# Turning attention probabilities eight at a time instead of four in a streaming Conformer layer

## Chip, cores and metric

One core of a Trainium2 chip runs the whole layer. The metric is device time in microseconds (us) of one execution; a version is timed several times and compared by the median.

## What is computed

One layer of a streaming encoder over 2048 prompt frames and 64 sample frames of width 1024, all in float32: a normalised input goes through one projection into a gated pair for a convolution branch, queries, keys and values, and two gates; the two branches are merged by the gates, projected and added; a gated feed-forward part follows. The attention branch is banded: each chunk of 64 frames reads itself and the 8 chunks before it, with 8 heads of 64 channels.

```python
q = rms_norm(q.reshape(B, T, N_HEADS, HEAD_DIM), p['q_norm_g'])
k = rms_norm(k.reshape(B, T, N_HEADS, HEAD_DIM), p['k_norm_g'])
o = attend(q, k, v, p['rel_bias']).reshape(B, T, ATTN_DIM)
...
s = jnp.einsum('bqhd,bkhd->bhqk', q, k).astype(jnp.float32) * ATTN_SCALE
s = s + rel_bias[:, rel].astype(jnp.float32)[None]
s = jnp.where(mask[None, None], s, NEG_INF)
p = jax.nn.softmax(s, axis=-1).astype(v.dtype)
return jnp.einsum('bhqk,bkhd->bqhd', p, v)
...
merged = jax.nn.sigmoid(g_conv) * conv_out + jax.nn.sigmoid(g_attn) * attn_out
x = x + gt1 * (merged @ p['w_o'])
```

## The kernel before

**Number format.** TensorE multiplies float32 data as a high part and a rest, so a projection step is a triple of matmuls (high by high, rest by high, high by rest; in the trace `ps<-hh,whi`, `ps<-hl,whi`, `ps<-hh,wlo`, or the same with the operands exchanged). A tile that TensorE is to read is split first: ScalarE copies it into the rounded high part, VectorE subtracts that from the source and writes the rest.

**Stages.** Phase one (0 to about 1163 us of the span) takes the prompt in four blocks of frames (0 to 3), each with its norm, its projections for queries, keys, values, gated pair and gates, the convolution and the attention of 8 heads; block 0 has the 8 sample heads too. Between the blocks of projections some steps of the modulation (`pa<-wmod,cl`) are put. Phase two merges the branches (`ps<-cin`, gated tiles `t<-tg,ps`), projects, and runs the feed-forward part. Attention results go to DRAM as `o_d`, the convolution's normalised channels (`ln`) as `c_d`; both are split into the tiles `part_h` and `part_l` by `parts()`, a ring of two buffers that the storing of normalised keys uses too. Tiles of phase two take memory of phase one, so the first of them wait for the last stores.

**What sets the order.** The program is written out by Python generators. Each attention head is a generator `attend(i)` in a lane; while the projections are being written, `stream.tick` lets lanes put in a step whenever a model of the engines' load says that the step's inputs are ready. A bare `yield` gives the projections the next turn; `yield t` waits until the model's TensorE time reaches `t`. In phase one TensorE runs in the order in which the kernel writes its matmuls (a schedule given by hand for that engine alone); the order on VectorE, ScalarE, GpSimd (POOL) and SyncE (SP) is set by the tile scheduler.

**One prompt head.** For four tiles of 128 queries: scores (`sc<-kk,q`, one PSUM tile), reduction with bias on VectorE (`pr,sm<-sc,bias`), exponential and scaling on ScalarE. Then the probabilities are turned: for each group `jj` in `seq`, TensorE transposes up to four 128 x 128 pieces of `pr` into one PSUM tile `ptp`, `split` copies it into `ph` and `pl` (three buffers each), and the group goes to the list `pend`. `av` multiplies a group with the values into `po`. Heads of blocks 1 to 3 have five groups of four transposes (`seq` 3, 4, 0, 1, 2); heads of block 0 have four groups of 4, 3, 2 and 1. `ptp` shares a pool of five PSUM banks (tag `gp`) with the projections `ps`, the norm's and the keys' transposes `pt`, and the modulation's `pa`.

**Keys.** Each key tile is normalised (`kn<-kn,r` on VectorE), transposed on TensorE (`pt<-ident,kn`) at least 5 us of model time later, split and stored.

**Lines.** Every compute instruction is recorded through a helper, so all of them have line L105 in the trace, and the tiles' names tell them apart. L1350 stores the convolution's channels, L1460 a pair of heads.

Of the kernel before, what the change touches and what calls it, by code (L numbers as in the profile page):

```python
# [8 lines left out]
F32 = mybir.dt.float32  # L9
# [7 lines left out]
P = 128  # L17
# [605 lines left out]
def streaming_layer(ctx: ExitStack, tc: tile.TileContext, I, O):  # L623
    nc = tc.nc
    stream = Stream()
    pe, dve, act, gps = (
        Meter(e, n, stream) for e, n in ((nc.tensor, "pe"), (nc.vector, "dve"), (nc.scalar, "act"), (nc.gpsimd, "pool"))
    )
# [28 lines left out]
    ident = const.tile([P, P], F32, name="ident")  # L657
# [118 lines left out]
    ps_g = p1.enter_context(tc.tile_pool(name="ps_g", bufs=5, space=PSUM))  # L776
# [6 lines left out]
    def temp(name, shape=(P, 512)):  # L783
        return wk.tile(list(shape), F32, tag="t", name=name, bufs=NT)
# [679 lines left out]
    def spans(b):  # L1464

        if b == "s":
            return 0, SMP, 0, CACHE + SMP
        past = QB if b else 0
        return SMP + QB * b, QB, CACHE + SMP + QB * b - past, QB + past
# [19 lines left out]
    def fetch_qk(i):  # L1489
        if i < len(order) and ("qk", i) not in now:  # L1490
            x, h = order[i]
            if spare["open"]:
                spare["heads"].append(i)
            now["qk", i] = load_qk(x, h, *spans(x))

    def fetch(i):
        if i < len(order) and i not in loaded:
            x, h = order[i]
            fetch_qk(i)
            if now["bias"] is None or now["bias"][0] != h:  # L1500
                now["bias"] = h, load_bias(h)
            first = not i or x not in ("s", 0, order[i - 1][0])
            lag = FIRST_LAG if first else QK_LAG
            loaded[i] = max(stream.load["pe"] + BIAS_LAG, ahead_qk.get(i, stream.load["pe"] + lag))

    def fetch_v(i):
        if i < len(order) and ("v", i) not in now:
            x, h = order[i]
            now["v", i] = load_v(h, *spans(x)[2:])

    def attend(i):
        x, h = order[i]
        q0, nq, k0, nk = spans(x)
        yield lambda: now["scored"] == i - 1
        fetch(i)
        fetch_v(i)
        if not i:
            fetch_qk(1)
        yield loaded[i]
        if i + 1 < len(order) and (spare["open"] or i in spare["heads"]):  # L1520
            fetch_qk(i + 1)
            ahead_qk[i + 1] = stream.load["pe"] + QK_LAG
        (q2, kk), (_, bias), vnow = now["qk", i], now["bias"], now["v", i]
        tiles = []
        for t in range(0, nq, P):
            n = min(P, nq - t)
            if x not in (0, "s"):
                ps = ps_a.tile([P, 2, 512], F32, tag="s", name="sc")
                for j in range(2):
                    for d in range(2):  # L1530
                        pe.matmul(ps[:, j, :320], q2[:, d, t : t + P], kk[:, t + 320 * j : t + 320 * j + 320], start=d == 0, stop=d == 1)
                w, src, bs = 640, ps[:, :, :320], bias[:, ::-1]
            else:
                w = nk if x == "s" else t + P

                if "banks" not in now:
                    sc = ps_a.tile([P, 2, 512], F32, tag="s", name="sc")
                    now["banks"] = [sc[:, 0:1], sc[:, 1:2]]
                ps = now["banks"].pop(0)
                now["banks"].append(ps)  # L1540
                for d in range(2):
                    pe.matmul(ps[:n, 0, :w], q2[:, d, t : t + n], kk[:, :w], start=d == 0, stop=d == 1)
                src, bs = ps[:n, 0:1, :w], bias[:n, 64:384][:, ::-1] if x == "s" else bias[:, :w][:, ::-1]
            pr, sm, free, ready = softmax_max(src, n, w, bs)
            tiles.append((pr, sm, n, w))
            if t + P < nq:
                yield free + PE_LAG, SCORE_ROOM
            else:
                fetch(i + 1)
                if (x, order[min(i + 2, len(order) - 1)][0]) in ((0, 0), ("s", "s")):  # L1550
                    fetch_qk(i + 2)
                now["scored"] = i
            if t:
                softmax_scale(*tiles[-2], x in ON_ACT)
        yield ready
        softmax_scale(*tiles[-1], x in ON_ACT)
        yield stream.when("act" if x in ON_ACT else "dve") + PE_LAG
        while now["finished"] < i - 1:
            yield lambda: now["finished"] == i - 1
        fetch_v(i + 1)  # L1560
        po = ps_a.tile([P, 512], F32, tag="o", name="po")
        if x == "s":
            pt = ps_g.tile([P, 512], F32, tag="gp", name="ptp")
            ph = wk.tile([P, 512], F32R, tag="ph", name="ph", bufs=3)
            pl = wk.tile([P, 512], F32R, tag="pl", name="pl", bufs=3)
            js = ((0, P), (1, P), (2, SMP))
            for j, m in js:
                c = slice(j * SMP, j * SMP + SMP)
                pe.transpose(pt[:m, c], tiles[0][0][:SMP, j * P : j * P + m], ident[:SMP, :SMP])
            stream.after("act", "pe")  # L1570
            split(ph[:, : 2 * SMP], pl[:, : 2 * SMP], pt[:, : 2 * SMP])
            split(ph[:SMP, 2 * SMP : 3 * SMP], pl[:SMP, 2 * SMP : 3 * SMP], pt[:SMP, 2 * SMP : 3 * SMP])
            yield stream.when("dve") + PE_LAG
            for j, m in js:
                c = slice(j * SMP, j * SMP + SMP)
                for y_ in (ph, pl):
                    pe.matmul(po[:, :SMP], vnow[:m, j], y_[:m, c], start=j == 0 and y_ is ph, stop=j == 2 and y_ is pl)
        else:
            seq = (0, 1, 2, 3) if x == 0 else (3, 4, 0, 1, 2)

            def av(jj, ph, pl, _):
                if x:
                    uses = [(jj, 0, min(jj, 3) + 1)] + ([(jj + 5, jj + 1, 4)] if jj < 3 else [])
                else:
                    uses = [(jj, jj, 4)]
                for j, a, e in uses:
                    for y_ in (ph, pl):
                        pe.matmul(
                            po[:, a * P : e * P], vnow[:, j], y_[:, a * P : e * P], start=jj == seq[0] and y_ is ph,
                            stop=jj == seq[-1] and y_ is pl and j == uses[-1][0], skip_group_check=True,  # L1590
                        )

            pend = []
            for jj in seq:
                if len(pend) > 2:
                    yield pend[0][3] + PE_LAG
                    av(*pend.pop(0))
                pt = ps_g.tile([P, 512], F32, tag="gp", name="ptp")
                t0 = 0 if x else jj
                for t in range(t0, 4):  # L1600
                    j = (jj - t + (5 if t > jj else 0)) if x else jj
                    pe.transpose(pt[:, t * P : t * P + P], tiles[t][0][:, j * P : j * P + P], ident)
                ph = wk.tile([P, 512], F32R, tag="ph", name="ph", bufs=3)
                pl = wk.tile([P, 512], F32R, tag="pl", name="pl", bufs=3)
                stream.after("act", "pe")
                w = 512 - t0 * P
                if x in ON_POOL and jj % 2:
                    p32 = temp("p32")
                    act.activation(p32[:, :w], pt[:, t0 * P :], AF.Copy)
                    act.activation(ph[:, t0 * P :], p32[:, :w], AF.Copy)  # L1610
                    stream.after("pool", "act")
                    gps.tensor_tensor(pl[:, t0 * P :], p32[:, :w], ph[:, t0 * P :].bitcast(F32), ALU.subtract)
                    pend.append((jj, ph, pl, stream.when("pool")))
                else:
                    split(ph[:, t0 * P :], pl[:, t0 * P :], pt[:, t0 * P :])
                    pend.append((jj, ph, pl, stream.when("dve")))
                yield
            for args in pend:
                yield args[3] + PE_LAG
                av(*args)  # L1620
        yield stream.when("pe")
        yield from finish_head(h, po, SMP if x == "s" else QB, q0, "s" if x == "s" else "p")
        now["finished"] = i
# [95 lines left out]
    ps_g = ctx.enter_context(tc.tile_pool(name="ps_c", bufs=4, space=PSUM))  # L1719
# [184 lines left out]
    for s, (lo, hi) in enumerate(CBLOCKS):  # L1904
        tiles = token_tiles(lo, hi)
# [476 lines left out]
```

## Time and profile before

| | |
|---|---|
| median of three runs | 2945.97 us (2940.69 to 2946.77) |
| profiled execution | 2941.67 us |
| its span, instructions | 2939.5 us, 44832 |
| mean granted TensorE clock | 0.997 |
| busy: PE, DVE, ACT, POOL | 98%, 70%, 46%, 40% |

PE is TensorE's matmuls, PEld its weight loads, DVE VectorE, ACT ScalarE. A row of the timeline has the start in us from the span's start, the length in us, the engine, the line, the operation and its tiles as output<-inputs, the shape, and how many instructions are run together; brackets hold the idle time before it and what ended that.

### The profile page before, as it was taken

The numbers are of one execution on the slowest core, as the hardware profiler recorded it, in microseconds if no ns is written. First come the engines' busy times: TensorE is split into PE (matmuls) and PEld (weight loads), VectorE is DVE, ScalarE is ACT, GpSimd is POOL, SyncE is SP. The second block draws the span as 40 slices with busy tenths as digits, with TensorE's granted clock in tenths as the row PEclk, the third lists the DMA queues.
The fourth block names the chain that finished last, engine by engine and source line by source line (L and its number), as shares of the span: only waits on it lengthen the run. The fifth ranks groups of instructions, "written<-read, shape, count | busy, mean of one in ns | idle before, by whom it ended". The sixth has DMA issues, their size and how long they took to land.

```text
span 2939.5 us, 44832 instructions
## 1 busy us (share of the span) xinstructions
PE 2889.3 (98%) x16193; PEld 2587.5 (88%) x16193; DVE 2053.9 (70%) x3648; ACT 1362.7 (46%) x2453; POOL 1164.9 (40%) x753
## 2 busy tenths in 40 slices
PE   7999999999999999999999999999999999999999
PEld 5899777888888887988999998999999999999998
DVE  5897788668967885577777756666666557566666
ACT  3346543751564266563444345444444345444442
POOL 1201210111011002553566452366567742465667
PEclk9999999999999999999999999999999999999999
DMA  9989899978996987984444875332333965333333
GB/s 322 315 305 314 287 281 329 285 232 306 285 297 197 320 270 224 291 295 157 144 144 146 292 261 200 97 122 94 115 115 104 346 220 179 97 103 106 115 107 127
DMA packets 467067, 628.04 MB, mean 214 GB/s; under 512 B 36196, under 2 KB 314584, under 8 KB 466845
## 3 DMA queue, kind: packets, MB, share of 16 engines
q1 hardware_dynamic: 452944, 606.11, 63.4%
q10 hardware_dynamic: 13901, 19.08, 1.9%
q8 instruction: 127, 2.08, 0.3%
q14 instruction: 95, 0.78, 0.1%
HBM read 476.53 MB, written 148.54 MB: 213 GB/s over the span
## 4 chain that ended last, share of the span: by engine, by line
PE 47%; DVE 2%; ACT 1%; DMA 1%; issue 1%; POOL 0%; SPq 0%; ACTq 0%; DVEq 0%; POOLq 0%
PE ps L105 29%; PE pd L105 13%; PE pw L105 5%; DVE wlo L105 1%; ACT whi L105 1%; DVE ps L105 0%; DMA cin<-o_d 0%; DMA x<-x_d 0%; DVE acc L105 0%; ACT xn L105 0%; DMA wst<-in_w_ffn_in 0%; DMA wfo<-in_w_ffn_out 0%; DMA tg<-g_d 0%; DVE sums L105 0%; PE pt L105 0%
## 5 line engine op out<-in xcount | busy, mean ns | idle before, releaser
L105 PE MATMUL ps<-t,whi 128*128 128x384 f32 (+1 forms) x2112 | 502.0, 322 | 2.8 <-ACT u L105 1.7
L105 POOL TENSOR_TENSOR wlo<-wst,whi 128x1024 fp32r<-128x1024 f32 (+1 forms) x159 | 362.7, 2293 | 246.1 <-ACT whi L105 214.4
L105 ACT ACTIVATE whi<-wst 128x1024 fp32r<-128x1024 f32 (+1 forms) x265 | 258.3, 979 | 316.1 <-PE ps L105 129.6
L105 PE MATMUL ps<-b,whi 128*128 128x384 f32 (+1 forms) x1584 | 380.7, 325 | 6.4 <-DVE v L105 2.1
L105 PEld LDWEIGHTS ps<-t,whi 128*128 128x128 f32 x2112 | 367.8, 188 | 10.1 <-ACT u L105 3.9
L105 DVE SCALAR_TENSOR_TENSOR y<-u,wd,y 128x512 f32<-128x512 f32 (+1 forms) x480 | 370.1, 774 | 8.0
L105 PE MATMUL ps<-hh,whi 128*128 128x512 f32 (+2 forms) x992 | 362.8, 366 | 0.1
L105 DVE TENSOR_TENSOR acc<-acc,pd 128x512 f32<-128x512 f32 x482 | 322.2, 685 | 48.1 <-PE pd L105 45.6
L105 PE MATMUL ps<-hh,wlo 128*128 128x512 f32 (+2 forms) x992 | 345.2, 348 | 0.0
L105 PE MATMUL ps<-hl,whi 128*128 128x512 f32 (+2 forms) x992 | 344.5, 347 | 0.0
L105 PE MATMUL ps<-t,wlo 128*128 128x384 f32 (+1 forms) x1056 | 338.5, 321 | 0.0
L105 PE MATMUL pd<-whi,hid 128*128 128x512 f32 x912 | 297.9, 391 | 0.6 <-DVE hid L105 0.3
L105 PEld LDWEIGHTS ps<-b,whi 128*128 128x128 f32 x1584 | 276.9, 188 | 14.6 <-DVE v L105 3.2
L105 ACT ACTIVATE pr<-pr,sm 128x640 f32<-128x640 f32 (+3 forms) x272 | 201.9, 749 | 137.1 <-DVE sm L105 134.8
L105 PE MATMUL ps<-b,wlo 128*128 128x384 f32 (+1 forms) x792 | 256.1, 323 | 0.0
L105 POOL TENSOR_TENSOR r<-t,mhalf 128x1 f32<-128x1 f32 (+2 forms) x68 | 82.3, 1219 | 403.7 <-DVE t L105 377.8
L105 PEld LDWEIGHTS ps<-hh,wlo 128*128 128x128 f32 x992 | 186.5, 188 | 22.6
L105 DVE TENSOR_TENSOR wlo<-wst,whi 128x1024 fp32r<-128x1024 f32 (+1 forms) x106 | 135.9, 1286 | 100.3 <-ACT whi L105 98.9
L105 PEld LDWEIGHTS pd<-whi,hid 128*128 128x128 f32 x912 | 171.2, 188 | 37.2 <-DVE acc L105 1.8
L105 PEld LDWEIGHTS ps<-hh,whi 128*128 128x128 f32 x992 | 187.0, 189 | 18.2 <-issue 3.3
L105 PEld LDWEIGHTS ps<-hl,whi 128*128 128x128 f32 x992 | 187.4, 189 | 14.3 <-issue 1.7
L105 PEld LDWEIGHTS ps<-t,wlo 128*128 128x128 f32 x1056 | 198.2, 188 | 0.8
(233 smaller groups left out, 6309.6 us busy)
## 6 DMA issues: line engine op xcount, KB each, us to landing
whi<-w_din_h SPq DMA_DIRECT2D x72, 512.0 KB, 6.4
wlo<-w_din_l SPq DMA_DIRECT2D x72, 512.0 KB, 7.3
wst<-sum_d SPq DMA_DIRECT2D x131, 256.0 KB, 3.1
wfo<-in_w_ffn_out SPq DMA_DIRECT2D x64, 512.0 KB, 4.1
wmod<-in_w_ada SPq DMA_DIRECT2D x46, 512.0 KB, 8.8
sum_d<-ws SPq DMA_DIRECT2D x88, 256.0 KB, 2.0
wst<-in_w_ffn_in SPq DMA_DIRECT2D x85, 256.0 KB, 3.2
wst<-in_w_in SPq DMA_DIRECT2D x40, 512.0 KB, 6.0
```

Source lines behind the costliest of these rows:

```text
L105: self.last = f(*args, **kw)
```

## The change

The transposes of two groups are put into TensorE's order back to back, in two PSUM tiles, and both are split before the head gives up its turn: runs of eight, of seven and three in block 0, and of four for a fifth group alone. `turned` holds the second tile of a pair. The list of waiting groups is shortened before a new pair: if two groups wait, and the group to come has not been turned and is not the last, the oldest is multiplied first. A head of blocks 1 to 3 has three turns instead of five, one of block 0 two instead of four. Which transposes, splits and products there are stays the same.

```diff
-            pend = []
+            def turn_probs(jj):
+                pt = ps_g.tile([P, 512], F32, tag="gp", name="ptp")
+                for t in range(0 if x else jj, 4):
+                    j = (jj - t + (5 if t > jj else 0)) if x else jj
+                    pe.transpose(pt[:, t * P : t * P + P], tiles[t][0][:, j * P : j * P + P], ident)
+                return pt
+
+            pend, turned = [], {}
             for jj in seq:
-                if len(pend) > 2:
+                if len(pend) > 2 or len(pend) == 2 and jj not in turned and jj != seq[-1]:
                     yield pend[0][3] + PE_LAG
                     av(*pend.pop(0))
-                pt = ps_g.tile([P, 512], F32, tag="gp", name="ptp")
-                t0 = 0 if x else jj
-                for t in range(t0, 4):
-                    j = (jj - t + (5 if t > jj else 0)) if x else jj
-                    pe.transpose(pt[:, t * P : t * P + P], tiles[t][0][:, j * P : j * P + P], ident)
+                if jj not in turned:
+                    turned.update({i: turn_probs(i) for i in seq[seq.index(jj) :][:2]})
+                pt, t0 = turned.pop(jj), 0 if x else jj
                 ph = wk.tile([P, 512], F32R, tag="ph", name="ph", bufs=3)
                 pl = wk.tile([P, 512], F32R, tag="pl", name="pl", bufs=3)
...
-                yield
+                if not turned:
+                    yield
```

Since a head's steps come at other times, the steps of the other lanes move too, and the tile scheduler sets other orders on the other engines. Three places follow.

TensorE in block 2, one head before the change:

```order
L105 MATMUL ptp<-ident,pr 128x128 x4
L105 MATMUL ps<-hh,whi 128x512
L105 MATMUL ps<-hl,whi 128x512
L105 MATMUL ps<-hh,wlo 128x512
L105 MATMUL ptp<-ident,pr 128x128 x4
L105 MATMUL ps<-hh,whi 128x512
L105 MATMUL ps<-hl,whi 128x512
L105 MATMUL ps<-hh,wlo 128x512
L105 MATMUL ptp<-ident,pr 128x128 x4
```

The start of the same kind of head after it:

```order
L105 MATMUL ptp<-ident,pr 128x128 x8
L105 MATMUL ps<-hh,whi 128x512
L105 MATMUL ps<-hl,whi 128x512
L105 MATMUL ps<-hh,wlo 128x512
L105 MATMUL ps<-hh,whi 128x512
L105 MATMUL ps<-hl,whi 128x512
L105 MATMUL ps<-hh,wlo 128x512
L105 MATMUL ps<-hh,whi 128x512
L105 MATMUL ps<-hl,whi 128x512
L105 MATMUL ps<-hh,wlo 128x512
L105 MATMUL po<-ph,vv 128x512
L105 MATMUL po<-pl,vv 128x512
```

Eight transposes stand together, and the first product follows three projection triples behind them.

VectorE at the seam between block 0 and block 1, before (names carry their buffers' numbers; kn_4027 is the key tile that TensorE transposes first, kn_4095 a later one):

```order
L105 TENSOR_TENSOR kn_4095<-kn_4095,r_4166 128x512
L105 ISA pr_4254,sm_4255<-sc_1921,bias_194 128x384
L105 ISA sm_4255 128x1
L105 TENSOR_SCALAR u_4131<-tb_4183,ps_4185 128x512
L105 RECIPROCAL sm_4243<-sm_4243 128x1
L105 TENSOR_SCALAR y_4130<-u_4131,wd_178,cols_175 128x512
L105 RECIPROCAL sm_4255<-sm_4255 128x1
L105 COPY R_4276<-pa_4259 128x256
L105 TENSOR_TENSOR part_l_4119<-ln_4114,part_h_4118 128x512
L105 TENSOR_TENSOR part_l_4127<-ln_4122,part_h_4126 128x512
L105 TENSOR_SCALAR part_l_4152<-pt_4146,gqk_179,part_h_4151 128x512
L105 TENSOR_TENSOR kn_4027<-kn_4027,r_4041 128x512
```

VectorE there after the change (kn_4126 is the last of the three key tiles, which now come in TensorE's order):

```order
L105 ISA pr_4209,sm_4210<-sc_1921,bias_194 128x256
L105 ISA sm_4210 128x1
L105 RECIPROCAL sm_4210<-sm_4210 128x1
L105 ISA pr_4231,sm_4232<-sc_1921,bias_194 128x384
L105 ISA sm_4232 128x1
L105 TENSOR_TENSOR kn_4126<-kn_4126,r_4159 128x512
```

The key tile stands directly behind the reduction of a 128 x 384 score tile, where before eleven instructions stood between the reduction's neighbour kn_4095 and kn_4027.

TensorE at the same seam after the change:

```order
L105 MATMUL pt_4298<-ident_160,kn_4126 128x128 x4
L105 MATMUL ptp_4308<-ident_160,pr_4167 128x128
L105 MATMUL ptp_4308<-ident_160,pr_4209 128x128
L105 MATMUL ptp_4308<-ident_160,pr_4231 128x128
L105 MATMUL ptp_4308<-ident_160,pr_4261 128x128
L105 MATMUL ptp_4313<-ident_160,pr_4209 128x128
L105 MATMUL ptp_4313<-ident_160,pr_4231 128x128
L105 MATMUL ptp_4313<-ident_160,pr_4261 128x128
L105 MATMUL pa_4326<-wmod_610,cl_192 32x256 x4
L105 MATMUL pa_4326<-wmod_612,cl_192 32x256 x4
```

A pair of four and three transposes follows the key tile's, and the modulation's first matmul stands directly behind the pair.

VectorE at the end of phase one, before:

```order
L105 TENSOR_TENSOR pl<-ptp,ph 128x512 x5
L105 TENSOR_TENSOR o_p<-other,po 64x512
L105 TENSOR_SCALAR y<-y,cols 128x512
L105 TENSOR_SCALAR ln<-ln,y 128x512
L105 TENSOR_TENSOR part_l<-o_p,part_h 128x512
L105 TENSOR_TENSOR part_l<-ln,part_h 128x512
L105 TENSOR_SCALAR ps<-tg,ps 128x320
L105 TENSOR_TENSOR part_l<-ln,part_h 128x512
L105 TENSOR_SCALAR t_12594<-tg,ps 128x320
```

And after:

```order
L105 TENSOR_SCALAR y<-y,cols 128x512
L105 TENSOR_SCALAR ln<-ln,y 128x512
L105 TENSOR_TENSOR pl<-ptp,ph 128x512 x2
L105 COPY row<-pt 32x128
L105 TENSOR_TENSOR pl<-ptp,ph 128x512 x3
L105 TENSOR_TENSOR o_p<-other,po 64x512
L105 TENSOR_TENSOR part_l<-o_p,part_h 128x512
L105 TENSOR_TENSOR part_l<-ln,part_h 128x512
L105 TENSOR_SCALAR ps<-tg,ps 128x320
L105 TENSOR_SCALAR t_12594<-tg,ps 128x320
```

One `part_l<-ln` stands behind the last head's result `o_p` where two stood.

## Prediction

> **What bounds the kernel now.** I read the page first, then TensorE's waits in the stretch that holds the changed step, a table of stretches, and the timeline where TensorE waits long. Busy time and the chain of waits:
>
> ```profile
> span 2939.5 us, 44832 instructions
> PE 2889.3 (98%) x16193; PEld 2587.5 (88%) x16193; DVE 2053.9 (70%) x3648; ACT 1362.7 (46%) x2453; POOL 1164.9 (40%) x753
> PE 47%; DVE 2%; ACT 1%; DMA 1%; issue 1%; POOL 0%; SPq 0%; ACTq 0%; DVEq 0%; POOLq 0%
> ```
>
> TensorE is busy for 98% of the span and holds the chain wherever it has an owner. The change takes no matmul from it, so it can only win or lose where TensorE waits or runs slowly. Columns of the table: length, busy us (instructions) of each engine, granted clock, DMA share, GB/s.
>
> ```profile
> core 0: us, PE busy (x) PEld busy (x) DVE busy (x) ACT busy (x) POOL busy (x), PEclk, DMA share, GB/s
> 345.00:365.00 20.00, 16.04 (x95) 11.88 (x93) 12.69 (x30) 8.38 (x20) 0.55 (x2) 0.91 0.89 298
> 365.00:385.00 20.00, 20.00 (x94) 16.71 (x93) 18.99 (x37) 8.21 (x18) 3.64 (x2) 0.91 0.94 289
> 600.00:1110.00 510.00, 509.32 (x2777) 430.81 (x2775) 395.46 (x749) 243.30 (x445) 57.10 (x51) 1.00 0.85 274
> 1150.00:1160.00 10.00, 9.28 (x51) 7.50 (x50) 5.81 (x13) 9.03 (x17) 2.37 (x1) 1.00 0.25 86
> 1170.00:1175.00 5.00, 1.87 (x13) 1.61 (x11) 2.62 (x2) 0.00 (x0) 1.82 (x1) 0.89 0.43 134
> 1175.00:1185.00 10.00, 9.71 (x49) 9.71 (x50) 3.73 (x10) 2.88 (x4) 3.18 (x2) 0.71 0.95 297
> ```
>
> From 600 to 1110 us, where most of the regrouped heads run, TensorE idles 0.68 us in 510: nothing is to be had there. Two places are left, the seam between the first two blocks of frames (345 to 385) and the step from attention into the merge (1160 to 1185). TensorE's waits between 180 and 1260 (total, times, longest) name them:
>
> ```profile
> PE pt L105 <- DVE kn L105: 4.0, 1, 4.0
> PE ps L105 <- DVE t L105: 3.4, 1, 3.4
> PE pa L105 <- DMA wmod<-in_w_ada: 2.6, 4, 0.7
> PE po L105 <- DVE pl L105: 0.8, 3, 0.3
> PE ptp L105 <- ACT pr L105: 0.7, 2, 0.5
> ```
>
> Only the first two are followed by a lower clock (0.91 twice; 0.71).
>
> **The change, part by part. (a) The grouping.**
>
> ```profile
> 781.74 0.60 PE L105 MATMUL ptp<-ident,pr 128*128 128x128 f32 x4
> 782.87 0.60 PE L105 MATMUL ptp<-ident,pr 128*128 128x128 f32 x4
> ...
> 784.58 0.39 PE L105 MATMUL ps<-hh,whi 128*128 128x512 f32 x1
> ...
> 785.28 0.39 PE L105 MATMUL ps<-hh,whi 128*128 128x512 f32 x1
> 1137.79 1.03 PE L105 MATMUL ptp<-ident,pr 128*128 128x128 f32 x8
> 1139.36 0.60 PE L105 MATMUL ptp<-ident,pr 128*128 128x128 f32 x4
> ```
>
> Four transposes and a projection triple take 782.87 − 781.74 = 1.13 us from start to start, a triple alone 785.28 − 784.58 = 0.70, so four transposes cost 0.43. Eight stand together once already: with a triple 1139.36 − 1137.79 = 1.57, so eight cost 0.87 = 2 × 0.435. The 64 runs that disappear are worth 64 × (0.87 − 2 × 0.43) = 0.6 us at the rounding of the rows, either way. I take 0.
>
> **(b) The wait for kn goes.** The key heads' tiles kn leave VectorE in the opposite order to the one TensorE wants:
>
> ```profile
> 353.04 0.69 DVE L105 TENSOR_TENSOR kn<-kn,r 128x512 f32<-128x512 f32 x1
> 359.68 0.68 DVE L105 TENSOR_TENSOR kn<-kn,r 128x512 f32<-128x512 f32 x1
> 360.51 0.63 PE L105 MATMUL pt<-ident,kn 128*128 128x128 f32 x4 [3.96 <-DVE kn L105]
> ```
>
> The transposes at 360.51 take the tile written at 359.68; the one of 353.04 is wanted only later. In the changed order VectorE writes the three kn tiles in TensorE's order, and the last one directly behind a score reduction, 24 projection matmuls ahead of its use: 8 triples × 0.70 = 5.6 us, against 0.69 for the multiply. So the 3.96 goes, and what would be late next is the split in (c). The clock was 0.91 over two stretches of 20 us, which costs up to 2 × 20 × 0.09 = 3.6. Together −7.6; ends −7.6 and 0 (if VectorE reaches that multiply 6 us late).
>
> The Trainium skill ("TensorE: Matmul & The Clock Gate", Part 1) has the gate fall to half clock after an idle window of about 3.4 us and rise after a busy one as long. The trace agrees that only the waits of 3.96 and 3.42 were followed by a lower clock. By that rule an estimate of each loss is half of 3.4, or 1.7, not the rows' 3.6 and 2.9, and the sum below would be 3.1 weaker: 2938.4.
>
> **(c) A new wait at the same seam.** In the changed order TensorE there runs four kn transposes, then a pair of four and three probability transposes, and directly behind them the first matmul pa of the next modulation step, which takes the PSUM bank of the pair's first tile. That bank is free after its split, a ScalarE copy and a VectorE subtraction (durations shortest/median/longest, in ns):
>
> ```profile
> L105 ACT ACTIVATE ph<-ptp x168: 199/584/609, 194.4 to 1161.2; 128x512 fp32r<-128x512 f32 x128, 128x128 fp32r<-128x128 f32 x16, 128x384 fp32r<-128x384 f32 x8, 128x256 fp32r<-128x256 f32 x8
> L105 DVE TENSOR_TENSOR pl<-ptp,ph x168: 205/687/693, 196.4 to 1161.8; 128x512 fp32r<-128x512 f32 x128, 128x128 fp32r<-128x128 f32 x16, 128x384 fp32r<-128x384 f32 x8, 128x256 fp32r<-128x256 f32 x8
> ```
>
> 0.58 + 0.69 = 1.27, of which three transposes (0.33) cover a part: 0.94. If each engine first finishes one more operation of about 0.6 to 0.7, it is 2.4. I take +1.7. Queued behind that matmul is all of TensorE's order. VectorE also gets this work some 3 us earlier, in a stretch where the next block's projections wait for its norm tiles:
>
> ```profile
> 337.54 0.50 PE L105 MATMUL ps<-whi,hl 128*128 128x512 f32 x1 [0.63 <-DVE hl L105]
> ```
>
> I take +1 (0 to +3) for a longer wait of that kind.
>
> **(d) The last head.**
>
> ```profile
> 1152.59 0.74 PE L105 MATMUL sc<-kk,q 128*128 128x320 f32 x4
> 1157.02 1.20 PE L105 MATMUL ptp<-ident,pr 128*128 128x128 f32 x9 [0.50 <-ACT pr L105]
> ```
>
> From its last scores to the transposes that need them is a chain of 1157.02 − 1152.59 = 4.4 us. Now four triples lie between; then nine, 9 × 0.70 = 6.3 us, so the 0.50 goes. Against that, eight transposes stand before the last triple, and their splits queue behind each other. −1.0 (0 to −1.5).
>
> **(e) The start of the merge.**
>
> ```profile
> 1164.57 0.56 PE L105 MATMUL ps<-cin,whi 128*128 128x320 f32 x2 [1.40 <-DVE o_p L105]
> 1165.86 0.68 DVE L105 TENSOR_TENSOR part_l<-o_p,part_h 128x512 fp32r<-128x512 f32 x1
> 1166.57 0.32 SPq L1460 DMA_DIRECT2D o_d<-part_l  x1
> 1169.59 2.79 DVE L105 TENSOR_TENSOR part_l<-ln,part_h 128x512 fp32r<-128x512 f32 x1 [0.70 <-DMA o_d<-part_l]
> 1169.43 2.39 POOL L105 TENSOR_TENSOR wlo<-wst,whi 128x1024 fp32r<-128x1024 f32 x1 [5.71 <-ACT whi L105]
> 1172.40 0.32 SPq L1350 DMA_DIRECT2D c_d<-part_l  x1
> 1174.75 0.49 DVE L105 SCALAR_TENSOR_TENSOR t<-tg,ps 128x320 f32<-128x320 f32 x1 [2.38 <-DMA c_d<-part_l]
> 1171.57 0.31 PE L105 MATMUL ps<-cin,wlo 128*128 128x320 f32 x1
> 1175.29 0.90 PE L105 MATMUL ps<-cin,whi 128*128 128x320 f32 x2 [3.42 <-DVE t L105]
> ```
>
> Today two channel groups of the convolution's norm remain behind the last head. The second needs the ring buffer part_l that the head's result is just being stored from, so it starts at 1169.59, runs 2.79 beside a POOL subtraction instead of 0.68, is stored at 1172.40, and the tile t, which reuses memory of these last stores, waits until 1174.75. TensorE stands 3.42 for t. In the changed order one such group is left; it follows the head's own part_l at once, into the other buffer. It would end near 1166.5 + 0.7, and with the same 2.35 from issue to t (1174.75 − 1172.40) t could start near 1170, before TensorE runs dry at 1171.6 + 0.3. What would be late next is the same store stretched by POOL, which leaves up to 0.9. The wait and the clock after it (10 × 0.29 = 2.9) are 6.3; less 0.5, the middle of that rest: −5.8 (−3 to −6.3).
>
> **(f) Steady state.** A pair's first product po stands behind four more transposes and about three triples, 0.43 + 2.1 = 2.5 us, where three or four groups covered it before; its split needs 1.27 and more where the engines are occupied (VectorE 395 of 510). Today's po waits are 0.8 in all. I take +1.0 (0 to +3).
>
> Sum: 0 − 7.6 + 1.7 + 1.0 − 1.0 − 5.8 + 1.0 = −10.7. The profiled execution took 2941.67 (span 2939.5 and 2.2 around it), 4.3 below the median of the three runs, 2945.97; I subtract from both: 2931.0 for a profile, **2935.3 for the median**. The merge and feed-forward behind 1185 keep their work.
>
> **Rivals.** *1. Only one long wait goes.* The chain at the seam runs through VectorE's order and loaded engines, the one at the merge through two stores and POOL; for it: either needs several microseconds of cover to hold. Without (b) the sum is −3.1, without (e) −4.9: 2941 to 2943, not distinguishable from no change. Chance 0.20.
>
> *2. Slower: the pair starves PSUM.* A pair holds two of the five banks that transposes share with the projections, and frees the second only after two copies and a subtraction, 2 × 0.58 + 0.69 = 1.9 us, longer beside other work; projections or po would stand behind splits at each of the 64 pairs. At 0.3 us each that is +19: 2945.97 − 10.7 + 19 = 2954. For it speaks that the seam in (c) shows just this; against it that three triples cover the first split. It decides from (10.7 + 5.9) / 64 = 0.26 us a pair. Chance 0.20.
>
> *3. The clock falls at the seam after all.* Eleven transposes (11 × 0.108 = 1.2 us) and a wait of up to 2.4 stand together there. If transposes do not hold the clock up, that is 3.6 without a projection matmul, like today's 3.96, and the 3.6 of clock come back: −7.1, 2938.9. Against it: twelve transposes in a row around 1157.02 kept the clock at 1.00 (stretch 1150 to 1160). Chance 0.05. The Trainium skill ("TensorE: Matmul & The Clock Gate", Part 4) states that transposes do not count as TensorE-busy in the same way, which speaks against longer runs; that stretch does not show it.
>
> **How the numbers follow.** The forecast, both waits gone, has 0.55; its own range is 2928 to 2941, from the ends of (b) to (f), of which not all come together. About 0.2%, 5.9 us, can be told from no change. Faster: the forecast but for 0.03, and rival 3: 0.57. Same: 0.03 and most of rival 1: 0.20. Slower: rival 2 and the rest of rival 1: 0.23. Low end 2926: both waits gone and the runs' own spread (2940.7 to 2946.8) favourable. High end 2952: most of rival 2 up to 0.26 us a pair and somewhat over it; beyond lie about 0.1 above and 0.05 below.
>
> **What would show it.** Right: no kn wait over 1 us, a pa wait for pl of 1 to 2.4 us in its place, clock 1.00 from 345 to 385; one part_l<-ln behind the last o_p, no wait for t, 1.00 from 1175 to 1185; still under 2 us of idle from 600 to 1110. Wrong: a new TensorE wait over 3 us with a lower clock behind it, a fall in the last stretch of phase two, or po and ps waits for pl in the hundreds of nanoseconds at most pairs (rival 2).

## The result, and the profile after

The changed kernel takes 2956.13 us (median of five, 2953.42 to 2957.41) against 2945.32 for the kernel before: ratio 1.0042, 95% interval 1.0029 to 1.0054. It is slower by 10.8 us. Its profiled execution has a span of 2954.0 us, 14.5 more than before, and the head of its page shows that TensorE has not been given more to do:

```profile
span 2954.0 us, 44847 instructions
PE 2888.2 (98%) x16193; PEld 2585.8 (88%) x16193; DVE 2047.6 (69%) x3648; ACT 1358.5 (46%) x2453; POOL 1165.9 (39%) x753
```

2888.2 us busy against 2889.3: what grew is the time between. The waits of TensorE from 180 to 1260 us, in the same view as before:

```profile
PE sc L105 <- DVE sm L105: 7.5, 7, 4.7
PE po L105 <- DVE pl L105: 4.9, 5, 1.4
PE sc L105 <- DMA kk<-k_d: 4.8, 3, 2.6
PE pt L105 <- DVE x_t L105: 2.7, 1, 2.7
PE pa L105 <- DVE pl L105: 1.4, 1, 1.4
PE ps L105 <- DVE t L105: 0.9, 1, 0.9
```

The two waits on which the forecast stood have changed as forecast: kn (4.0) is gone, t went from 3.4 to 0.9. But scores `sc` now wait 7.5 us for the reduction before them, where it was 2.7, and 4.8 us for their keys, where it was nothing; `po` waits 4.9, where it was 0.8; and a norm tile x_t comes 2.7 late. The stretches:

```profile
180.00:600.00 420.00, 401.08 (x2389) 347.09 (x2388) 316.31 (x652) 218.93 (x464) 58.29 (x58) 0.98 0.89 293
320.00:330.00 10.00, 7.27 (x30) 5.67 (x29) 7.12 (x22) 6.66 (x17) 3.93 (x5) 0.83 0.85 282
360.00:370.00 10.00, 8.58 (x71) 6.33 (x70) 8.57 (x17) 3.26 (x7) 0.21 (x1) 1.00 0.84 262
380.00:390.00 10.00, 5.27 (x23) 3.83 (x21) 7.28 (x18) 2.49 (x8) 1.64 (x1) 0.76 0.98 285
390.00:400.00 10.00, 10.00 (x40) 8.31 (x39) 7.66 (x18) 4.45 (x13) 0.00 (x0) 0.73 0.25 67
600.00:1110.00 510.00, 507.56 (x2784) 430.58 (x2783) 394.73 (x749) 234.75 (x436) 54.74 (x49) 1.00 0.83 269
1175.00:1185.00 10.00, 8.52 (x57) 7.94 (x56) 4.46 (x7) 4.43 (x7) 2.54 (x2) 1.00 0.64 238
1185.00:1195.00 10.00, 9.05 (x61) 8.63 (x59) 3.79 (x10) 0.98 (x3) 1.81 (x1) 1.00 0.77 226
1195.00:1205.00 10.00, 8.07 (x45) 6.68 (x45) 5.21 (x11) 4.89 (x6) 7.09 (x3) 1.00 1.04 348
```

The same stretches before, as far as they weren't shown, and one more in which the clock was lower:

```profile
180.00:600.00 420.00, 409.80 (x2464) 354.75 (x2463) 322.94 (x664) 222.41 (x468) 57.71 (x58) 0.99 0.91 299
360.00:370.00 10.00, 9.49 (x36) 8.17 (x37) 6.64 (x14) 3.13 (x6) 0.00 (x0) 0.66 1.05 384
470.00:480.00 10.00, 9.27 (x52) 7.02 (x45) 5.69 (x14) 2.58 (x6) 0.00 (x0) 0.83 0.98 378
```

From 180 to 600 us TensorE idles 420 - 401.1 = 18.9 us after the change and 10.2 before. From 600 to 1110, where most regrouped heads run, it idles 2.4 and 0.7. The change costs little where most of its pairs are, and much around the heads of block 0. The largest of the new waits there, by rows of SyncE, VectorE and TensorE:

```profile
375.14 1.92 SPq L249 DMA_DIRECT2D wmod<-in_w_ada  x4
377.15 1.09 SPq L1473 DMA_DIRECT2D bias<-rb_d  x2
380.22 0.33 PE L105 MATMUL sc<-kk,q 128*128 128x128 f32 x2
387.59 0.29 DVE L105 CUSTOM_DVE_ANT_0 pr<-sc,bias 128x128 f32<-128x128 f32 x1 [2.65 <-DMA bias<-rb_d]
387.95 0.80 PE L105 MATMUL sc<-kk,q 128*128 128x256 f32 x2 [4.73 <-DVE sm L105]
```

The bias of the next heads is loaded at 377.15, right behind four modulation tiles, and VectorE can first use it 10.4 us later, at 387.59. TensorE multiplies the first score tile at 380.22, 3.1 us after the issue, but it can't be reduced before the bias is there, and the second score tile, which needs the same PSUM tile, holds TensorE for 4.73 us; the clock is 0.76 and 0.73 in the two stretches of 10 us there. Before the change the same scores came 8 us after the load, and nobody waited:

```profile
378.66 1.19 SPq L1473 DMA_DIRECT2D bias<-rb_d  x2
386.73 0.33 PE L105 MATMUL sc<-kk,q 128*128 128x128 f32 x2
389.21 0.28 DVE L105 CUSTOM_DVE_ANT_0 pr<-sc,bias 128x128 f32<-128x128 f32 x1
```

Two more loads come late for their scores, the keys of block 1's first heads and those of the last head:

```profile
485.69 0.44 SPq L1430 DMA_DIRECT2D kk<-k_d  x1
495.50 0.82 PE L105 MATMUL sc<-kk,q 128*128 128x320 f32 x4 [1.86 <-DMA kk<-k_d]
...
1155.05 0.82 PE L105 MATMUL sc<-kk,q 128*128 128x320 f32 x4 [2.64 <-DMA kk<-k_d]
```

### The profile page after: what moved, and what is told of

Read it like the earlier page. It is cut to its first block, busy times and chain, and to the rows that moved or that the text cites. A ratio compares the mean times of both kernels' runs of the same rounds, so it can differ in the third digit from the quotient of the medians.

```text
span 2954.0 us, 44847 instructions
## 1 busy us (share of the span) xinstructions
PE 2888.2 (98%) x16193; PEld 2585.8 (88%) x16193; DVE 2047.6 (69%) x3648; ACT 1358.5 (46%) x2453; POOL 1165.9 (39%) x753
## 4 chain that ended last, share of the span: by engine, by line
PE 47%; DVE 2%; ACT 1%; issue 1%; DMA 0%; POOL 0%; ACTq 0%; DVEq 0%; POOLq 0%
PE ps L105 29%; PE pd L105 14%; PE pw L105 5%; DVE wlo L105 1%; ACT whi L105 0%; DVE pw L105 0%; DVE ps L105 0%; DVE t L105 0%; DMA wst<-in_w_ffn_in 0%; DVE acc L105 0%; DMA tg<-g_d 0%; PE pt L105 0%; POOL ws L105 0%; ACT xn L105 0%; DVE sums L105 0%
```

## Experiments

Three theories were tested, against a fourth. **Loads:** the next heads' loads stand behind bulk loads, and that place is what costs. **Turns:** heads in fewer turns run faster than the loads and the other lanes' work around them. **Run** (the expectations also call it banks): eight transposes in a row, in two banks, cost as such; its weaker form is that the early product does. Against all of them stands **order**: any other order costs. Ratios are to the kernel before, timed on the same chip, with 95% intervals.

### Which heads

The changed function with the pair, and the condition on `pend`, for block 0 only (`x == 0`) and for blocks 1 to 3 only:

```diff
+                    turned.update({i: turn_probs(i) for i in seq[seq.index(jj) :][: 1 if x else 2]})   # block 0
+                    turned.update({i: turn_probs(i) for i in seq[seq.index(jj) :][: 2 if x else 1]})   # blocks 1 to 3
```

> Pairs of groups in block 0's eight heads alone (16 of the 64 pairs); heads of blocks 1 to 3 turn four at a time as before. SyncE's order at the two seams is that of the changed kernel. Loads theory: the waits at 388 and 495 us are there in full with their clock, the merge and the later heads as before: 2948 to 2954. Banks theory: a quarter of the 10.8 us, 2947 to 2949. My prediction's own terms for this part, the kn wait gone and the pa wait there (-7.6 + 1.7 + 1), would give 2940.

Measured 2961.54 us, 1.0063 (1.0047 to 1.0079). No theory had given so much.

> Pairs in the 24 heads of blocks 1 to 3 alone (48 of the 64 pairs); block 0 turns its groups singly as before, so SyncE's order at the first two seams is that of before. Loads theory: no wait of more than 2 us for bias or keys at the seams, the kn wait of 3.96 us stays, the keys' wait near 1155 us may come: 2944 to 2949. Banks theory: three quarters of the 10.8 us, 2952 to 2955.

Measured 2946.94 us, 1.0010 (1.0002 to 1.0019). A quarter of the pairs, those of block 0, costs 17.6 us, and three quarters cost 3.0. That is against the run theory at its root: 48 pairs cost 3.0 us together, 0.06 a pair. In the second kernel the kn wait is back at 4.0 us and the keys' wait near the end is there (1.92 us at 1143).

### Where the loads stand

The release of modulation tiles 12 us of model time later, in the changed kernel and in that before:

```diff
-        self.stream.at(self.stream.when("pe"), lambda n=self.given: self.free(n), True)
+        self.stream.at(self.stream.when("pe") + (12000.0 if self.stream.load["pe"] > 200e3 else 0.0), lambda n=self.given: self.free(n), True)
```

> The changed kernel with one edit: between the blocks of frames, the refill of a used modulation weight tile is issued 12 us of model time later. TensorE's order stays that of the changed kernel; on SyncE the loads of bias, queries and keys now stand ahead of the refills at the two places where TensorE's new waits at 387.95 (4.73 us) and 495.50 us (1.86 us) stand. Loads theory (a head's loads, issued close behind the four refills of 0.5 MB each, land some 10 us after issue and the scores wait): both waits go, and most of the clock lost from 385 to 600 us (0.98 over 215 us, 4.3 us) with them; 2956.1 becomes 2945 to 2949. Banks theory (each pair costs TensorE something at every head): 2954 to 2958. Order theory (any change of order moves the time a few us up or down with no one cause): no number, 2948 to 2962.

Measured 2959.33 us, 1.0046 (1.0033 to 1.0059): no gain.

> The kernel before with the same edit, the refills 12 us of model time later. TensorE's order stays that of before; on SyncE two of the four refills now stand right ahead of the bias load at the first seam, and three of four right ahead of the queries' and keys' loads at the start of block 1's heads. Loads theory: new waits of up to 2 us each at scores there, 2945.3 becomes 2945 to 2951. Banks theory: no change, 2943 to 2947.

Measured 2950.30 us, 1.0023 (1.0014 to 1.0032). The time lies in the loads theory's range, but not for its reason. The waits of the scores are those of the kernel before (2.2 us in four from 180 to 600); what came is a wait for the late modulation weights themselves:

```profile
471.30 1.08 PE L105 MATMUL pa<-wmod,cl 128*32 128x256 f32 x8 [3.38 <-DMA wmod<-in_w_ada]
```

And the changed kernel with only the first of these refills late (the same edit, with `200e3 < self.stream.load["pe"] < 340e3`):

> The changed kernel with the refill of four modulation tiles 12 us of model time later at the first seam alone, so that the bias, query and key loads of the next heads stand ahead of it; nothing moves near 476 us, and TensorE's order is that of the changed kernel. Loads theory: the wait at 388 us falls from 4.7 to about 2 us, as with the refills all late, without the new wait of 4.7 us for a refill at 479 us; with the clock 2949 to 2953. If that wait isn't worth its length: 2955 to 2958.

Measured 2954.78 us, 1.0042 (1.0027 to 1.0057). What became of the waits, by TensorE's rows of the first and then of the third kernel:

```profile
479.48 0.73 PE L105 MATMUL pa<-wmod,cl 128*32 128x256 f32 x8 [4.73 <-DMA wmod<-in_w_ada]
```

```profile
386.77 0.50 PE L105 MATMUL sc<-kk,q 128*128 128x256 f32 x2 [1.98 <-DVE sm L105]
495.94 1.02 PE L105 MATMUL sc<-kk,q 128*128 128x320 f32 x4 [3.57 <-DMA kk<-k_d]
```

The wait at 388 us fell from 4.73 to 1.98 as expected, in both. With all refills late the next modulation step missed its weights for 4.73 us; with one late, the scores at 496 waited 3.57 us for their keys, where it was 1.86 in the changed kernel. The DMA engines are busy for 0.89 to 0.91 of the stretch from 180 to 600 us in these kernels, and each time a wait that was shortened at one load came back at another. The loads theory in its narrow form, that the place behind the four refills is what costs, falls.

### Turns, product and controls

A yield after every group in block 0, so that heads there keep four turns: with pairs in block 0 only, then in the whole change, then with a yield after every group in all blocks.

```diff
-                if not turned:
-                    yield
+                yield                          # pairs in block 0 only; and all blocks
+                if not (x and turned):         # whole change, block 0 only
+                    yield
```

> Pairs in block 0 alone, with the early product, but with a yield after each group as before, so a head keeps four turns: eight transposes stand together, the second split is given out one turn later. Run theory: the 17 us stay, 2954 to 2962. Turns theory: near before, 2943 to 2949. Order theory: in between, 2945 to 2956.

Measured 2947.19 us, 1.0007 (0.9997 to 1.0017). The pairs stand as before and only the turns differ, so of the 17.6 us 14.2 go with the two turns. The number lies in the range of the turns theory, and in that of the order theory as well.

> The change, with a yield after each group in block 0 alone; the heads of blocks 1 to 3 have three turns as in the change. If the parts add up (3.4 us for pairs with four turns in block 0, 3.0 for the change in blocks 1 to 3): 2948 to 2952. If the heads of blocks 1 to 3 lose because block 0 ended otherwise: 2954 and more.

Measured 2944.91 us, 1.0007 (0.9997 to 1.0016): the whole change but for block 0's turns, no slowdown that can be told from none, and less than the sum of the parts.

> The change in all four blocks, but with a yield after each group, so that heads keep four and five turns; 64 runs of eight or seven stand as in the change. Turns theory: 2943 to 2949. Run theory (the eight in a row and their two banks cost): 2953 to 2958. My prediction's sum has no term for the turns and would give 2935 for both.

Measured 2952.68 us, 1.0037 (1.0024 to 1.0050). This one missed the turns theory's number, and the run theory's by little. Block 0 cost next to nothing in it (by the 2850th of the 4200 projection matmuls, with block 1's heads done, it is 1.1 us behind the kernel before, counted from 180 us); the time went in the last block, where the last head's steps now came late. TensorE's rows there:

```profile
1165.70 0.55 PE L105 MATMUL ptp<-ident,pr 128*128 128x128 f32 x3 [1.01 <-ACT pr L105]
1186.14 0.90 PE L105 MATMUL ps<-cin,whi 128*128 128x320 f32 x2 [4.09 <-DVE t L105]
```

The early product alone, and two turns without it:

```diff
# kernel before
-                if len(pend) > 2:
+                if len(pend) > 2 or not x and len(pend) == 2 and jj == seq[2]:
# pairs in block 0
-                if len(pend) > 2 or not x and len(pend) == 2 and jj not in turned and jj != seq[-1]:
+                if len(pend) > 2:
```

> The kernel before, with one part of the change alone and in block 0 alone: the oldest group is multiplied before the third group when two wait; groups are still turned four at a time, four turns a head. Early-product theory (this condition moves the heads): most of the 17 us that pairs in block 0 cost, 2954 to 2962. Turns theory (two turns a head instead of four bring the heads' later steps and loads into a full stretch) and run theory (eight transposes in two banks, first split close to its product): within 3 us of before, 2942 to 2948. Order theory (any other order of block 0 costs something, because that of before happens to fit): 2945 to 2956.

Measured 2948.06 us, 1.0014 (1.0004 to 1.0024).

> Pairs in two turns in block 0 alone, without the early product: the oldest group is multiplied when three wait, between the two splits of the second pair. Turns theory (two turns are what costs): 2954 to 2963. If it takes both, two turns and the early product, to bring the cost (the early product alone cost 4.3 us): 2945 to 2950.

Measured 2954.57 us, 1.0036 (1.0025 to 1.0048). So of the 17.6 us in block 0, two turns without the early product bring 11.0, the early product without two turns 4.3.

Two controls with other orders and none of the change (`ATTN_NS` 700 in place of 600; `PE_LAG` 500 in place of 400):

> Control: the kernel before, where only the least model time between two turns of attention is 700 ns and not 600; groups of four, four or five turns. It moves thousands of rows of TensorE's order and has none of the change. Order theory: slower by 4 to 17 us, 2948 to 2961, with new waits at the seams of the blocks. The other theories: within 3 us of before, 2941 to 2947.

Measured 2946.39 us, 1.0005 (0.9993 to 1.0017).

> Control: the kernel before, where only the lag that TensorE leaves after a split or a reduction is 500 ns of model time and not 400. Order theory: slower by 4 to 17 us, 2948 to 2961. The other theories: within 3 us of before, 2941 to 2947, or a little faster through shorter waits for splits.

Measured 2946.55 us, 1.0010 (1.0000 to 1.0020). In the first of them another kind of matmul stands at 3629 of the 16193 places of TensorE's order, in the change at 3468. So an order that differs as widely cost 2.6 us, and that an order differs is by itself no reason for 17.6. What one particular order costs is another question, as the controls below show.

### Slowing the heads down again

Scores held back after their loads, in blocks 0 to 2, for the changed kernel and that before; and in block 0 alone with pairs there (its condition is `x not in (0, "s")` in place of `x == 3`):

```diff
-            lag = FIRST_LAG if first else QK_LAG
-            loaded[i] = max(stream.load["pe"] + BIAS_LAG, ahead_qk.get(i, stream.load["pe"] + lag))
+            lag = FIRST_LAG if first else QK_LAG if x == 3 else 12000.0
+            loaded[i] = max(stream.load["pe"] + (BIAS_LAG if x == 3 else 10500.0), ahead_qk.get(i, stream.load["pe"] + lag))
...
-            ahead_qk[i + 1] = stream.load["pe"] + QK_LAG
+            ahead_qk[i + 1] = stream.load["pe"] + (QK_LAG if x == 3 else 12000.0)
```

> The changed kernel, in which scores of blocks 0 to 2 are held back until 12 us of model time after the loads of queries and keys and 10.5 us after that of the bias, in place of 9 and 6. Turns theory in its full form (a head in fewer turns ends sooner, so the next head's scores come as early as the lags allow and meet loads that take 10 us where the queue is full): no wait of TensorE for keys or a bias over 1 us before 1110 us; 2944 to 2950. If the loads are no part of the cost: 2953 to 2960.

Measured 2947.44 us, 1.0014 (1.0004 to 1.0023). The time came as the turns theory has it; its sign failed in one place, a wait of 2.1 us for a reduction between 460 and 520 us, whose bias was 1.7 us late.

> Pairs in two turns in block 0 alone (2961.5 us without this edit), scores of block 0 held back by the same lags; blocks 1 to 3 as before in turns and lags. Turns theory: the cost sits in block 0 and where its heads meet the loads, so most of the 17.6 us goes: 2944 to 2951. If block 0's two turns cost in another way than through early scores: 2955 to 2962.

Measured 2945.47 us, 1.0005 (0.9995 to 1.0014).

> Control for the held-back scores: the kernel before with the same lags (12 us after queries and keys, 10.5 us after the bias, in blocks 0 to 2). If the lags only undo what fewer turns brought: within 3 us of before, 2941 to 2947, since its scores rarely come that early. If they help any version by some 9 us: 2934 to 2938, and the 8.7 us that the changed kernel gained by them say nothing of the turns.

Measured 2952.87 us, 1.0029 (1.0019 to 1.0039). The lags bring the change from 10.8 us over the kernel before to 3.9 and block 0's pairs from 17.6 to 1.9, and cost the kernel before 9.3, which neither of the two theories had expected. So they are no help in themselves; but a lag alone, without the change, costs nearly as much as the change does. Nor does the wait for the bias explain the cost. VectorE's idle time for the tile `bias`, in the kernel before, the changed one, the changed one with scores held back, and the change with four turns in block 0:

```profile
DMA bias<-rb_d: 0.3, 2
```

```profile
DMA bias<-rb_d: 12.3, 3
```

```profile
DMA bias<-rb_d: 1.7, 1
```

```profile
DMA bias<-rb_d: 11.9, 3
```

The last of them is 1.4 us slower than the kernel before, the second 10.8, at nearly the same idle time of VectorE; the two turns without the early product have 3.8 us of it and are 11.0 slower.

Last, the changed kernel with heads of block 0 waiting at least 1.5 us after a pair:

```diff
-                    yield
+                    yield 0.0 if x else stream.load["pe"] + 1500.0
```

> The changed kernel, in which a head of block 0 waits at least 1.5 us of TensorE's model time after each pair before it goes on, so that its two turns take about as long as four; SyncE's order keeps the bias load right behind the four refills at the first seam. If the pace of block 0's heads is the cost, whatever sets it: 2945 to 2951. If only the loads that stand behind the refills are: 2954 to 2958.

Measured 2948.79 us, 1.0014 (1.0004 to 1.0023). Its bias load still stands behind the refills, and TensorE still waits 3.65 us for it, so most of the time came back elsewhere:

```profile
384.22 0.50 PE L105 MATMUL sc<-kk,q 128*128 128x256 f32 x2 [3.65 <-DVE sm L105]
```

### What they show together

Idle time of TensorE from 180 to 600 us (420 less its busy time) and what the clock took (for each 10 us, one less the granted clock) give an estimate of the lost time of each profiled execution. It counts a little twice where the clock is low while TensorE waits (about 1.4 us from 385 to 388 in the changed kernel). Beside it stand the change of that profiled execution and of the median. The column "place" is a measure of the heads' pace: how many of the 4200 projection matmuls of phase one TensorE starts, in the trace, before the last product of block 0's eighth head.

| kernel | place | idle | clock | sum | against before | profiled execution | median |
|---|---|---|---|---|---|---|---|
| before | 1920 | 10.2 | 5.1 | 15.3 | | | |
| the change | 1872 | 18.9 | 6.8 | 25.7 | +10.4 | +14.5 | +10.8 |
| pairs in block 0, two turns | 1872 | 20.5 | 13.6 | 34.1 | +18.8 | +33.7 | +17.6 |
| the same, no early product | 1839 | 20.1 | 6.8 | 26.9 | +11.6 | +13.1 | +11.0 |
| pairs in block 0, four turns | 1911 | 13.2 | 3.4 | 16.6 | +1.3 | +2.7 | +3.4 |
| the change, four turns in block 0 | 1911 | 13.3 | 0.0 | 13.3 | -2.0 | +1.3 | +1.4 |
| the change, scores held back | 1986 | 11.6 | 3.4 | 15.0 | -0.3 | +2.4 | +3.9 |
| pairs in block 0, scores held back | 1986 | 11.6 | 3.4 | 15.0 | -0.3 | +4.7 | +1.9 |
| the change, block 0 paced | 1884 | 12.6 | 3.4 | 16.0 | +0.7 | -0.9 | +4.5 |
| before, scores held back | 2037 | 17.0 | 6.8 | 23.8 | +8.5 | +11.0 | +9.3 |

Two rows are ends: the profiled execution of the pairs in block 0 took 2975.4 us, 14 more than its median, and that of the change with block 0 paced 2940.8, 8 less. Leaving out the first of these, the slower kernels of the table lose most of their time in this stretch.

Shown is where the loss sits and what it needs: the heads of block 0, and two turns in them. With four turns there, the pairs of block 0 cost 3.4 us and the whole change 1.4, neither of which can be told from none. Two turns do bring the heads forward: the eighth ends 48 projection matmuls, or 16 triples, earlier. But that the pace itself sets the cost is argued and not shown. For it speaks that every kernel whose eighth head ends at 1872 or earlier is 11 to 18 us slower, those with late refills (1872) among them, and that the others, with places from 1884 to 2037, cost 1 to 9. Against it speaks that the wait after a pair put that end back by only 12 matmuls, four triples, and still took 6.3 of the 10.8 us away, and that the kernel before with scores held back, the latest of all, costs 9.3. So a rival stays open: that this one order of block 0 merely falls badly.

Which of the waits there decides stays open too. It is never a single one: the kernels with the time back still wait some 2 to 4 us at 385 us or for x_t, as TensorE's rows of the change with four turns in block 0 show; but in that one no lower clock follows (1.00 in its row of the stretches).

```profile
324.75 0.44 PE L105 MATMUL pt<-ident,x_t 128*128 128x128 f32 x2 [2.49 <-DVE x_t L105]
385.41 0.50 PE L105 MATMUL sc<-kk,q 128*128 128x256 f32 x2 [2.04 <-DVE sm L105]
```

```profile
180.00:600.00 420.00, 406.73 (x2475) 353.14 (x2474) 319.06 (x667) 221.84 (x469) 59.52 (x58) 1.00 0.92 300
```

No version beats the kernel before: of sixteen, four can't be told from it (1.0005 to 1.0007), the interval of a fifth begins at 1.0000, and the others are slower. So the order theory holds in a weak form: other orders cost 0 to 9 us here, held-back scores in the kernel before 9.3, later refills alone 6.4, and only two turns in block 0 with nothing to hold its heads back reach 11 to 18.

## Why the prediction was wrong

The forecast was 2935.3 us, range 2926 to 2952; measured are 2956.1. The step that failed is in (b), in what it says would be late next, and behind it stands a cost that the sum put at nothing: what two turns instead of four do to the time at which block 0's heads meet the loads and the other lanes. By its own terms:

- **(a), grouping, 0.** Right. Blocks 1 to 3, with 48 of the 64 pairs, cost 3.0 us in all, and with four turns in block 0 all 64 pairs cost 1.4 (not told from none).
- **(b), the kn wait, -7.6.** The effect came: 3.96 of idle time is gone, and the clock from 360 to 370 us went from 0.66 to 1.00, worth 3.4. The step that failed stands in the same paragraph, "what would be late next is the split in (c)". What was late next and cost more was the bias for the next scores: 4.73 us, with a clock of 0.76 and 0.73 in those 20 us, worth up to another 5.1. From 345 to 400 us TensorE idles 6.7 us where it idled 5.2, at a clock of 0.91 where it was 0.94. By these numbers the place lost some 3.1, where (b) and the wait in (c) had it win 5.9. That this wait alone isn't the cost, the runs show too: with one refill late it was 1.98 us and the kernel took 2954.8. I had followed how VectorE's and TensorE's rows moved and not when the heads' loads on SyncE are issued against the scores that need them, though a head in two turns instead of four may ask for them sooner.
- **The clock.** "Only the first two are followed by a lower clock" misread the trace: in the kernel before the clock was also 0.83 from 470 to 480 us, behind four waits for modulation weights of at most 0.73 us. So the sum gave no clock price to new waits under 3 us, and the one for x_t had one. Of the two sizes weighed for the loss behind 3.96, the rows' 3.6 was near, since it was 3.4, and the 1.7 was half of it.
- **(c), the new wait for the pair's split, +1.7.** Right: 1.42 us, by TensorE's row:

```profile
363.38 0.85 PE L105 MATMUL pa<-wmod,cl 128*32 128x256 f32 x12 [1.42 <-DVE pl L105]
```

- **(c), later norm tiles, +1 (0 to +3).** Mis-sized: the x_t wait is 2.73 us, with a clock of 0.83 in that stretch for another 1.7; before, this kind of wait was 0.63.
- **(d), the last head, -1.0.** The 0.50 wait went, but its scores now wait 2.64 us for keys. The sign was wrong, and the term had counted 1.0 for a wait of 0.50.
- **(e), the merge, -5.8.** Mis-sized. The wait for t fell by 2.5 (3.42 to 0.94, at 1191.32 now), and the clock of 0.71 became 1.00 there (1185 to 1205). But the projection behind it then waited for its weights, 1.48 and 1.28 us at 1198.81 and 1210.32. From the first merge matmul (1164.57; 1179.55) to the first `ps<-t,whi` of the feed-forward part (1299.55; 1312.77) the gain is 135.0 - 133.2 = 1.8 us.

```profile
1191.32 0.56 PE L105 MATMUL ps<-cin,whi 128*128 128x320 f32 x2 [0.94 <-DVE t L105]
```

- **(f), products, +1.0 (0 to +3).** Too small: `po` waits 4.9 instead of 0.8, +4.1. Of it 2.8 is the second product of a pair's first group (0.91, 0.51 and 1.42 us at 518, 773 and 863), as the step describes.

Rival 2, the slower one, had the sign but neither the mechanism nor the place: a price at each of the 64 pairs is refuted by blocks 1 to 3. Rival 3 did not come: the clock at the seam's eleven transposes and wait is 1.00 (360 to 370). What was missing is a rival in which the heads' changed timing, not the transposes, costs the time; no step asked what fewer turns do to the lanes.

## What to carry to other kernels

In a kernel whose steps are dealt out by lanes, merging turns also brings the work forward (here the last head of block 0 by 16 triples); whoever merges them must ask for every load and every other lane's step that this moves, and not only for the instructions merged. In a stretch as full as this one (DMA share 0.91, VectorE busy for 323 of 420 us before the change), a removed wait is first worth the distance to the next late thing on the same path, so that one has to be found in all queues before the wait is counted as a gain. And split a change by where it acts before believing any mechanism: two runs showed that a quarter of the pairs carried the loss.

## What the runs showed of the hardware

Lower clock often came in steps of about 1.7 us of loss (0.83 or 0.66 in a stretch of 10 us), and not only behind waits as long as the two of the kernel before (3.96 and 3.42 us). The four waits of 0.56 to 0.73 us from 466 to 471 us there were followed by 0.83 (470 to 480). The wait of 2.73 us for x_t was followed by 0.83 in the changed kernel and by 1.00 in that with block 0 paced, whose wait is as long. Its row of the timeline, and of the stretches:

```profile
321.87 0.33 PE L105 MATMUL pt<-ident,x_t 128*128 128x128 f32 x1 [2.73 <-DVE x_t L105]
```

```profile
320.00:330.00 10.00, 7.71 (x43) 6.29 (x44) 8.90 (x25) 6.46 (x15) 3.10 (x3) 1.00 1.05 319
```

The Trainium skill ("TensorE: Matmul & The Clock Gate", Part 1) has a free-running window of about 3.4 us, which lets where a wait falls in it matter, and half clock for one window would be 1.7 us, an estimate from that page. The step agrees, and so does the half: the granted clock of the changed kernel is 0.50 from 388 to 395 us. That a wait of 2.7 us is enough is this case's own number. The loss by clock varied from 0 to 13.6 us in the same stretch between kernels with like work, as much as the idle time itself did.
